# An encoder block on one core: a tile of blocks in its own buffer, p's columns loaded by pairs, and stores of y from GpSimd's queue

## The chip, the core and the metric

The kernel runs on one core of a Trainium2 chip. The metric is the device time of one execution in microseconds (us); the median of several runs is compared. Five engines work from queues of their own: TensorE (PE, matmuls and transposes), VectorE (DVE), ScalarE (ACT), GpSimd (POOL) and SyncE (SP). SP issues most of the DMAs, in the order of its queue; an instruction at the head of a queue that waits holds back all behind it.

## What is computed

Two sequences (512 prompt tokens and 1,024 sample tokens, 1,024 channels, all fp32) go through one encoder layer with the same parameters:

```python
xn = rmsnorm(h, norm_mix_g);  z = xn @ w_in                # q, k, v, g_att, u, g_f
att = diff_attention(q, k, v, lam, rel_bias)               # 4 heads, two softmaxes each
att = rmsnorm(att, subln_g, 1e-5) * (1 - lambda_init) * silu(g_att)
fno = fourier_mix(u, w_fourier) * silu(g_f)                # 2-D DFT, real part, linear map
h = h + concatenate([att, fno]) @ w_out
h = h + sigmoid(rmsnorm(h, ple_norm_g) @ w_ple_gate) * (p @ w_ple_proj)
y = rmsnorm(h, final_norm_g)
```

The change lies in the last three lines: the output projection, the gate with the per-layer input p (256 columns per token), and the final norm.

## The kernel before

Each fp32 product is made of three fp32r matmuls: an operand is split into a high part (a cast on ACT) and a low part (a subtraction on DVE), and `hi*hi + hi*lo + lo*hi` is summed in PSUM. The 1,536 tokens make twelve rows of 128 (t = 0 to 3 prompt, 4 to 11 sample).

**Stages.** First come the input projections (to about 300 us) with the Fourier part, then attention head by head, with the remaining projections filled in between its steps (`all_fill`, L586, a generator that `pour` advances). The last things in that filling are the output projection of rows 0 and 1, done plainly (`project`, L569). What remains of the output projection, rows 2 to 11, is done after attention, two rows at a time (`project_pair`, L805), and then the gate, again two rows at a time (`front`, L881, and `gate_pair`, L944).

**A pair** is a 2x2 block product in Winograd's form: seven products of 128x512 by 512x512 instead of eight (`product`, L525: 12 matmuls each, 84 a pair). Its left operand is four blocks: c11 and c12 are the two halves of the first row's columns, c21 and c22 those of the second row's. Sums of them (`s1` to `s4`) are made on DVE, and each is split on ACT and DVE. The seven products go to four PSUM banks, and DVE adds each to the row x. Some banks are summed on after DVE has read them, so a product can wait for an addition to x. A finished row is stored to the DRAM buffer `hs[t]` and its sum of squares taken (`keep`, L559).

**The blocks' buffers.** `load_cl` (L535) loads a row's two blocks from `cT` with two DMAs of 256 KB, into two tags, `hi` and `lo`, of two buffers each (2 KB per partition each). Rows 0 and 1 take all four. Row 2 (the first pair's first row) gets its two when row 0's product is done, row 3 when row 1's is done: L609 is reached once for each of t = 0 and t = 1. Rows of x lie in the tag `x` of the pool `wo` (three buffers of 4 KB per partition), each fourth row in a fourth buffer (`row`, L792). Row 2's x is loaded in `all_fill` (L611).

**The gate.** `rows_in` (L859) loads one row x back from `hs[t]`, and its 128 columns of p (`p_cols`, 128 KB, in runs of 512 B) into one buffer `pr`, and splits them into `ph` and `pl` (two buffers each). `front` scales the row by its norm on ACT into a buffer `hn` (`normed`, L868; four buffers, shared with raw weights), turns it on PE (`turn`, L874), and makes the seven operands; the block called `al11` lies in the tag `lo`. `gate_pair` does the seven products and the four products with p (`per_layer`, L907). `finish_row` (L923) makes 1/rms (the power is done on POOL, L557), multiplies on DVE into the `hn` buffer (L933), and stores y from it in two halves of 256 KB (L935). The row's x buffer is free for the load of row t+4 once DVE has read it; the `hn` buffer is free for `normed` of row t+4 once the store of y has landed.

**Order.** The framework puts the instructions of each engine in an order of its own, from priorities and estimated times, and inserts the waits; it is not always the order of the program.

Of the kernel before, what the change touches and what calls it, by code (L numbers as in the profile page):

```python
# [10 lines left out]
F32 = mybir.dt.float32  # L11
F32R = mybir.dt.float32r
# [4 lines left out]
P = 128  # L17
KB = 8
# [4 lines left out]
NT = TT // P  # L23
# [9 lines left out]
def block_kernel(ctx, tc, i, yp, ys):  # L33


    nc = tc.nc
# [16 lines left out]
    def split(hi, lo, src, hi_eng="act", lo_eng="dve"):  # L53
        if hi_eng == "act":
            a = nc.scalar.copy(out=hi, in_=src)  # L55
        else:
            a = nc.vector.tensor_copy(out=hi, in_=src)
        eng = nc.vector if lo_eng == "dve" else nc.gpsimd
        return a, eng.tensor_tensor(out=lo, in0=src, in1=hi.bitcast(F32), op=ALU.subtract)  # L59
# [11 lines left out]
    qs, kh, kl, vv, ga, uu, yT, cT = {}, {}, {}, {}, {}, {}, {}, {}  # L71
# [14 lines left out]
    hs = [dram.tile([P, D], F32, name=f"hs{t}") for t in range(NT)]  # L86
# [6 lines left out]
    def x_rows(t):  # L93
        return i["x_prompt"][0, t * P:(t + 1) * P, :] if t < 4 else \
            i["x_sample"][0, (t - 4) * P:(t - 3) * P, :]
# [17 lines left out]
    ph = ctx.enter_context(tc.tile_pool(name="ph", bufs=1, reuse_waits="tile"))  # L113
# [139 lines left out]
    with tc.tile_pool(name="pn", bufs=1, side="right", reuse_waits="tile") as pn:  # L253
# [11 lines left out]
        def load_x(t):  # L265
            x = pn.tile([P, D], F32, tag="f4", name="x", bufs=5)
            return x, nc.sync.dma_start(out=x, in_=x_rows(t))
# [32 lines left out]
        for t in range(NT):  # L300
# [8 lines left out]
            lo = ph.tile([P, 512], F32R, tag="lo", name="lo", bufs=2)  # L309
# [33 lines left out]
        first = blocks(["k0", "q0"])  # L343
# [6 lines left out]
        for t in range(NT):  # L350
            ps = nat(t, wu)
            s, r = rows_of(t)
            u = px.tile([P, 512], F32, tag="th", name="u", bufs=3)
# [153 lines left out]

    wo, small = None, None
    wb = {}
    pair_cl, x2 = [], []  # L510

    def open_out():
        nonlocal wo, small
# [4 lines left out]
    def wblock(n, tag):  # L518


        pool = wo if tag[0] == "t" else pw
        wb[n] = tuple(pool.tile([P, 4, 512], F32R, tag=tag.replace("*", z), name=f"w{n}{z}") for z in "hl")
        return wb[n]
# [8 lines left out]
    def f4(name):  # L532
        return wo.tile([P, D], F32, tag=name, name=name, bufs=3)

    def load_cl(t, pair=False):  # L535
        cl = []
        for u in range(t, t + 2 if pair else t + 1):
            c, r = u // 4, (u % 4) * P
            for z, tag in enumerate(("hi", "lo")):
                cl.append(ph.tile([P, 4, P], F32R, tag=tag, name="cl", bufs=2))  # L540
                nc.sync.dma_start(out=cl[-1].bitcast(F32), in_=cT[c].rearrange(
                    "(k p) t -> p k t", p=P)[:, 4 * z:4 * z + 4, r:r + P])
        return cl
# [42 lines left out]
    def all_fill():  # L586
        yield from blocks(["k2", "q2", "g2", "k3", "q3", "g3"])
        yield from blocks(["f0", "f1", "f2", "f3"], (0, 1))
        last = blocks(["f0", "f1", "f2", "f3"], (2,))
        for n in ("11", "12", "21", "22"):  # L590
            wblock(n, f"x*{int(n[0]) - 1}{int(n[1]) - 1}")
        for k in range(KB):
            raw = px.tile([P, D], F32, tag="raw", name="raw", bufs=2)
            nc.sync.dma_start(out=raw, in_=i["w_out"][0][k * P:(k + 1) * P, :])
            for z in range(2):
                wh, wl = wb[f"{k // 4 + 1}{z + 1}"]
                split(wh[:, k % 4], wl[:, k % 4], raw[:, 512 * z:512 * z + 512],
                      lo_eng=("dve", "pool", "dve")[k % 3])
            next(last)
            yield  # L600
        early = [load_cl(t) for t in range(2)]
        yield from last
        open_out()
        for t in range(2):
            yield from project(t, early[t], load_x(t))
            if t == 0:
                for n in ("t4", "t1"):
                    load_sums(n)
            pair_cl.extend(load_cl(t + 2))  # L609
            yield  # L610
        x2.append(load_x(2))  # L611
        load_sums("t2")
        load_sums("t3")

# [165 lines left out]
    with ExitStack() as pcx:  # L780
        pool = pcx.enter_context(tc.tile_pool(name="pc", bufs=1, side="right", reuse_waits="tile"))
# [10 lines left out]
        def row(t):  # L792
            return pool.tile([P, D], F32, tag="x", name="x") if t % 4 == 3 else f4("x")
# [51 lines left out]
        for t in range(2, NT, 2):  # L845
            if t == 4:
                wp = [[pool.tile([P, D], F32R, tag=f"wp{k}{n}", name=f"wp{k}{n}") for n in "hl"]
                      for k in range(2)]
                gfin = pool.tile([P, D], F32, name="gfin")
                nc.scalar.dma_start(out=gfin, in_=i["final_norm_g"].rearrange(  # L850
                    "(a d) -> a d", a=1).broadcast_to([P, D]))
                for k in range(2):
                    raw = raw4()
                    nc.sync.dma_start(out=raw, in_=i["w_ple_proj"][0][k * P:(k + 1) * P, :])
                    split(*wp[k], raw)
            project_pair(t, pair_cl if t == 2 else load_cl(t, True),
                         [x2[0] if t == 2 else load_x(t, row(t)), load_x(t + 1, row(t + 1))])

        def rows_in(t):  # L859
            x = row(t)  # L860
            nc.sync.dma_start(out=x, in_=hs[t])
            pr = pool.tile([P, 2, P], F32, tag="pr", name="pr", bufs=1)
            nc.sync.dma_start(out=pr, in_=i["p_cols"].rearrange("(k p) t -> p k t", p=P)[:, :, t * P:(t + 1) * P])
            p2 = [pool.tile([P, 2, P], F32R, tag=f"p{n}", name=f"p{n}", bufs=2) for n in "hl"]
            split(*p2, pr)
            return x, p2

        def normed(t, x):  # L868
            hn = raw4()
# [9 lines left out]
            return bank.rearrange("p (a b) -> p a b", b=P)  # L879

        def front(t, rows=None):  # L881
            (xa, pa), (xb, pb) = rows or (rows_in(t), rows_in(t + 1))
            ga_, gb = normed(t, xa), normed(t + 1, xb)
            a = {n: halves(n) for n in SUMS}
            f21, f11 = (ph.tile([P, 4, P], F32, tag="hi", name="c", bufs=2) for _ in range(2))
            a["11"] = a["11"][0], ph.tile([P, 4, P], F32R, tag="lo", name="al11", bufs=2)
            f1, f2 = tmp(), tmp()
            nc.scalar.copy(out=f11, in_=turn(ga_, 0, tr()))
            split(*a["11"], f11)
            ps = turn(ga_, 1, tr())  # L890
            split(*a["12"], ps)
            nc.vector.tensor_tensor(out=f2, in0=ps, in1=f11, op=ALU.add)
            nc.scalar.copy(out=f21, in_=turn(gb, 0, tr()))
            ps = turn(gb, 1, tr())
            split(*a["22"], ps)
            add(f1, f21, ps)
            split(*a["s1"], f1)

            sub(f2, f2, f1)
            split(*a["s4"], f2)  # L900
            sub(f1, f1, f11)
            split(*a["s2"], f1)
            sub(f11, f11, f21)
            split(*a["s3"], f11)
            return (xa, xb), (pa, pb), (ga_, gb), a
# [17 lines left out]
        def finish_row(t, u, x, g, ss, n):  # L923
            x, g, last = x[u], g[u], t + u == NT - 1
            rs = pool.tile([P, 1], F32, tag="rs", name="rs", bufs=2)
            nc.vector.tensor_reduce(out=rs, in_=ss[:, 4 * u:4 * u + n], op=ALU.add, axis=mybir.AxisListType.X)
            rpow(rs, rs)
            t += u
            for z in range(2):
                w = slice(512 * z, 512 * z + 512)  # L930
                dst = yp[0, t * P:(t + 1) * P, w] if t < 4 else ys[0, (t - 4) * P:(t - 3) * P, w]
                if not last:
                    nc.vector.scalar_tensor_tensor(out=g[:, w], in0=x[:, w], scalar=rs, in1=gfin[:, w],  # L933
                                                   op0=ALU.mult, op1=ALU.mult)
                    nc.sync.dma_start(out=dst, in_=g[:, w])  # L935
                elif z == 0:
                    nc.scalar.mul(out=g[:, w], in_=x[:, w], mul=rs)
                    nc.scalar.dma_start(out=dst, in_=g[:, w])
                else:
                    nc.vector.tensor_scalar(out=g[:, w], in0=x[:, w], scalar1=rs, scalar2=None,  # L940
                                            op0=ALU.mult)
                    nc.sync.dma_start(out=dst, in_=g[:, w])
# [45 lines left out]
            finish_row(t, 1, x, g, ss, 3 if last else 2)  # L988


        first = [rows_in(t) for t in range(2)]
        for n, tag in (("11", "x*00"), ("21", "x*10"), ("t4", "t4*"), ("t1", "t1*"), ("t2", "x*01"),
                       ("22", "x*11"), ("t3", "t3*")):
            if n == "t1":
# [1 line left out]
            w = wblock(n, tag)  # L996
            for k in range(0, 4, 2):
# [11 lines left out]
                for m in range(2):  # L1009
                    g = gcol[:, 4 * j + k + m:4 * j + k + m + 1]  # L1010
# [79 lines left out]
```

## Time and profile before

| | us |
|---|---|
| median of 3 runs | 961.65 (960.3 to 963.35) |
| the profiled execution's own time | 964.62 |
| its span, first to last instruction | 962.8 |
| PE busy | 915.3 (95%) |
| VectorE busy | 637.5 (66%) |
| ScalarE busy | 449.6 (47%) |
| GpSimd busy | 98.5 (10%) |

The profile is of one execution. Times in its rows count from the span's start. A row in the timeline has start, duration, engine, line, operation, output<-inputs, and in brackets how long the engine had been idle before, and what ended that. The clock that TensorE was granted is given as a share of its full speed.

### The profile page before, as it was taken

The numbers are of one execution on the slowest core, as the hardware profiler recorded it, in microseconds if no ns is written. First come the engines' busy times: TensorE is split into PE (matmuls) and PEld (weight loads), VectorE is DVE, ScalarE is ACT, GpSimd is POOL, SyncE is SP. The second block draws the span as 40 slices with busy tenths as digits, with TensorE's granted clock in tenths as the row PEclk, the third lists the DMA queues.
The fourth block names the chain that finished last, engine by engine and source line by source line (L and its number), as shares of the span: only waits on it lengthen the run. The fifth ranks groups of instructions, "written<-read, shape, count | busy, mean of one in ns | idle before, by whom it ended". The sixth has DMA issues, their size and how long they took to land.

```text
span 962.8 us, 13087 instructions
## 1 busy us (share of the span) xinstructions
PE 915.3 (95%) x4536; PEld 747.7 (78%) x4536; DVE 637.5 (66%) x1230; ACT 449.6 (47%) x908; POOL 98.5 (10%) x123
## 2 busy tenths in 40 slices
PE   5999999999999999999999999899899998999995
PEld 4788888888887788888877887777678876777774
DVE  4676443057845698597776978973676777767674
ACT  5543311032324475365554656752343566555542
POOL 3100001010000111000112122421000000000000
PEclk9999999999999999999999999999899999999998
DMA  8669889255547844753577567648875471233211
GB/s 296 226 204 338 290 273 316 85 153 154 164 139 208 228 132 150 202 158 94 180 205 213 166 171 249 195 173 312 290 242 183 143 231 55 93 99 99 93 49 44
DMA packets 123315, 175.63 MB, mean 182 GB/s; under 512 B 9385, under 2 KB 76713, under 8 KB 122225
## 3 DMA queue, kind: packets, MB, share of 16 engines
q1 hardware_dynamic: 121280, 170.72, 55.7%
q0 software_dynamic: 1392, 2.63, 0.9%
q10 hardware_dynamic: 576, 1.44, 0.5%
q8 instruction: 36, 0.59, 0.3%
q14 instruction: 31, 0.25, 0.1%
HBM read 114.96 MB, written 59.80 MB: 182 GB/s over the span
## 4 chain that ended last, share of the span: by engine, by line
PE 72%; DMA 10%; DVE 9%; ACT 4%; issue 2%; SPq 1%; POOL 1%; POOLq 0%; DVEq 0%; ACTq 0%
PE acc L147 23%; PE bank L528 11%; PE sc L657 6%; PE acc L66 6%; PE acc L68 6%; PE acc L67 6%; PE tr L684 3%; DMA x<-hs 2%; DMA raw<-sg 2%; PE tr L67 2%; PE tr L66 2%; PE tr L68 2%; PE tr L414 1%; DMA raw<-w_in 1%; PE tr L284 1%
## 5 line engine op out<-in xcount | busy, mean ns | idle before, releaser
L147 PE MATMUL acc<-xh,wch 128*128 128x512 f32 x384 | 152.2, 396 | 0.0
L147 PE MATMUL acc<-xl,wch 128*128 128x512 f32 x384 | 152.1, 396 | 0.0
L147 PE MATMUL acc<-xh,wcl 128*128 128x512 f32 x384 | 151.7, 395 | 0.0
L663 ACT ACTIVATE pt<-pt,mx 128x1024 f32<-128x1024 f32 (+1 forms) x96 | 96.5, 1007 | 62.4 <-DVE mx L660 61.8
L660 DVE CUSTOM_DVE_ANT_0 pt<-sc,tb 128x1024 f32<-128x1024 f32 (+1 forms) x96 | 97.8, 1041 | 20.3 <-PE sc L657 13.6
L147 PEld LDWEIGHTS acc<-xh,wch 128*128 128x128 f32 x384 | 72.2, 188 | 13.7 <-issue 0.2
L147 PEld LDWEIGHTS acc<-xh,wcl 128*128 128x128 f32 x384 | 72.2, 188 | 13.4
L147 PEld LDWEIGHTS acc<-xl,wch 128*128 128x128 f32 x384 | 72.2, 188 | 13.1 <-issue 0.2
L66 PE MATMUL acc<-wnh,xh 128*128 128x512 f32 x192 | 77.1, 402 | 0.5 <-ACT wnh L55 0.5
L67 PE MATMUL acc<-wnl,xh 128*128 128x512 f32 x192 | 76.8, 400 | 0.0
L68 PE MATMUL acc<-wnh,xl 128*128 128x512 f32 x192 | 76.2, 397 | 0.0
L657 PE MATMUL sc<-kk,qq 128*128 128x512 f32 x160 | 65.7, 411 | 2.4 <-DMA kh_p<-hi 1.6
L657 PE MATMUL sc<-kll,qq 128*128 128x512 f32 x160 | 63.9, 399 | 0.0
L55 ACT CAST wth<-tr 128x512 fp32r<-128x512 f32 x80 | 45.4, 582 | 32.0 <-PE tr L684 31.8
L59 DVE TENSOR_TENSOR wtl<-tr,wth 128x512 fp32r<-128x512 f32 x80 | 53.5, 685 | 6.5 <-ACT wth L55 6.4
L679 DVE SCALAR_TENSOR_TENSOR pt<-pt,rc,pt 128x1024 f32<-128x1024 f32 (+1 forms) x48 | 56.0, 1166 | 1.1
L684 PE MATMUL tr<-ident,pt 128*128 128x128 f32 x320 | 48.4, 276 | 5.8 <-DVE g L729 4.2
L684 PEld LDWEIGHTS tr<-ident,pt 128*128 128x128 f32 x320 | 36.6, 140 | 17.1 <-DVE g L729 6.7
L705 POOL TENSOR_TENSOR g<-ot,g 128x256 f32<-128x256 f32 x24 | 20.3, 847 | 287.6 <-ACT ot L704 282.3
L66 PE MATMUL tr<-wth,v 128*128 128x256 f32 x160 | 45.6, 285 | 0.2 <-DVE wtl L59 0.2
L67 PE MATMUL tr<-wtl,v 128*128 128x256 f32 x160 | 45.5, 284 | 0.3 <-DVE wtl L59 0.2
L68 PE MATMUL tr<-wth,v 128*128 128x256 f32 x160 | 45.1, 282 | 0.0
(297 smaller groups left out, 2056.7 us busy)
## 6 DMA issues: line engine op xcount, KB each, us to landing
raw<-w_in SPq DMA_DIRECT2D x28, 512.0 KB, 5.1
x<-x_sample SPq DMA_DIRECT2D x16, 512.0 KB, 4.7
sot<-o SPq DMA_DIRECT2D x16, 512.0 KB, 4.1
cl<-cT SPq DMA_DIRECT2D x24, 256.0 KB, 3.8
hs<-x SPq DMA_DIRECT2D x12, 512.0 KB, 4.4
x<-hs SPq DMA_DIRECT2D x12, 512.0 KB, 3.8
x<-x_prompt SPq DMA_DIRECT2D x8, 512.0 KB, 5.2
wr<-w_out SPq DMA_DIRECT2D x8, 512.0 KB, 5.8
```

The costliest lines, as they stand in the source:

```text
L55: a = nc.scalar.copy(out=hi, in_=src)
L59: return a, eng.tensor_tensor(out=lo, in0=src, in1=hi.bitcast(F32), op=ALU.subtract)
L66: nc.tensor.matmul(out=out, lhsT=wh, rhs=xh, start=start, stop=False)
L67: nc.tensor.matmul(out=out, lhsT=wh, rhs=xl, start=False, stop=False)
L68: nc.tensor.matmul(out=out, lhsT=wl, rhs=xh, start=False, stop=stop)
L147: nc.tensor.matmul(out=ps, lhsT=a[:, k], rhs=b[c][k // 4][:, k % 4], start=(n == 0), stop=(n == 23))
L528: nc.tensor.matmul(out=out[:, w], lhsT=a[u][:, k], rhs=b[v][:, k, w], start=(start and k == 0 and n == 0), stop=(k == 3 and n == 2), skip_ ...
L657: nc.tensor.matmul(out=pss[c][:, n:n + 512], lhsT=qq[c], rhs=k[c][:, n:n + 512], start=(m == 0), stop=(m == 1))
L660: nc.vector.tensor_tensor_reduce(out=pt[c][:, :T], in0=ps[:, :T], in1=tb[:, off:off + T], scale=-1.0, scalar=3e38, op0=ALU.add, op1=ALU.mi ...
L663: nc.scalar.activation(out=pt[c][:, :T], in_=pt[c][:, :T], func=AF.Exp, scale=-1.0, bias=mx[:, c:c + 1], accum_out=sm[:, c:c + 1])
L679: nc.vector.scalar_tensor_tensor(out=pt[0][:, :T], in0=pt[1][:, :T], scalar=rc[:, 1:2], in1=pt[0][:, :T], op0=ALU.mult, op1=ALU.add)
L684: nc.tensor.transpose(out=ps[:, j * P:(j + 1) * P], in_=pt[0][:, (b + j) * P:(b + j + 1) * P], identity=ident)
```

## The change

Three edits. (1) After row 0's product, `all_fill` loads row 2's blocks as before, and row 3's two blocks with one DMA of 512 KB into a buffer of the tag `x` instead of into `hi` and `lo`; row 2's x is loaded in the pair's own step rather than in `all_fill`. (2) `rows_in` handles a pair of rows: it loads both rows x, reserves the gate's `al11` in the tag `lo`, and loads the pair's 256 columns of p with one DMA (runs of 1 KB) into the other `lo` buffer. (3) The stores of y of rows 0 to 9 are issued by GpSimd, those of rows 10 and 11 as before.

```diff
-    pair_cl, x2 = [], []
+    pair_cl = []
...
-            pair_cl.extend(load_cl(t + 2))
+            if t == 0:
+                pair_cl.extend(load_cl(2))
+                whole = wo.tile([P, KB, P], F32, tag="x", name="c3", bufs=3)
+                nc.sync.dma_start(out=whole, in_=cT[0].rearrange("(k p) t -> p k t", p=P)[:, :, 3 * P:4 * P])
+                pair_cl.extend([whole[:, 0:4], whole[:, 4:8]])
             yield
-        x2.append(load_x(2))
         load_sums("t2")
         load_sums("t3")
...
             project_pair(t, pair_cl if t == 2 else load_cl(t, True),
-                         [x2[0] if t == 2 else load_x(t, row(t)), load_x(t + 1, row(t + 1))])
+                         [load_x(t, row(t)), load_x(t + 1, row(t + 1))])
 
         def rows_in(t):
-            x = row(t)
-            nc.sync.dma_start(out=x, in_=hs[t])
-            pr = pool.tile([P, 2, P], F32, tag="pr", name="pr", bufs=1)
-            nc.sync.dma_start(out=pr, in_=i["p_cols"].rearrange("(k p) t -> p k t", p=P)[:, :, t * P:(t + 1) * P])
-            p2 = [pool.tile([P, 2, P], F32R, tag=f"p{n}", name=f"p{n}", bufs=2) for n in "hl"]
-            split(*p2, pr)
-            return x, p2
+
+            x = [row(t), row(t + 1)]
+            for u in range(2):
+                nc.sync.dma_start(out=x[u], in_=hs[t + u])
+            al11 = ph.tile([P, 4, P], F32R, tag="lo", name="al11", bufs=2)
+            pr = ph.tile([P, 2, 2 * P], F32, tag="lo", name="pr", bufs=2)
+            nc.sync.dma_start(out=pr, in_=i["p_cols"].rearrange("(k p) t -> p k t", p=P)[
+                :, :, t * P:(t + 2) * P])
+            p2 = []
+            for u in range(2):
+                p2.append([pool.tile([P, 2, P], F32R, tag=f"p{n}", name=f"p{n}", bufs=2) for n in "hl"])
+                split(*p2[u], pr[:, :, u * P:(u + 1) * P])
+            return x, p2, al11
...
-            (xa, pa), (xb, pb) = rows or (rows_in(t), rows_in(t + 1))
+            (xa, xb), (pa, pb), al11 = rows or rows_in(t)
...
-            a["11"] = a["11"][0], ph.tile([P, 4, P], F32R, tag="lo", name="al11", bufs=2)
+            a["11"] = a["11"][0], al11
...
-                    nc.sync.dma_start(out=dst, in_=g[:, w])
+                    (nc.gpsimd if t < NT - 2 else nc.sync).dma_start(out=dst, in_=g[:, w])
...
-        first = [rows_in(t) for t in range(2)]
+        first = rows_in(0)
```

## Rows read from the trace of the kernel before

**Rows 1.** Busy time by stretch: us, each engine's busy us, PE's granted clock, DMA share, GB/s
```profile
680.00:700.00 20.00, 18.76 (x68) 14.63 (x69) 15.46 (x24) 8.21 (x14) 0.00 (x0) 0.83 0.77 260
720.00:740.00 20.00, 20.00 (x89) 16.30 (x88) 13.03 (x23) 7.21 (x16) 1.64 (x3) 1.00 0.52 171
```

**Rows 2.** Timeline of PE, 655 to 720 us: the matmuls that it was idle before
```profile
672.58 0.49 PE L528 MATMUL bank<-w21h,ah 128*128 128x512 f32 x1 [1.82 <-ACT ah L55]
679.02 0.50 PE L528 MATMUL bank<-wt4h,ah 128*128 128x512 f32 x1 [2.62 <-ACT ah L55]
680.50 0.50 PE L528 MATMUL bank<-wt4h,al 128*128 128x512 f32 x1 [0.75 <-DVE al L59]
683.51 0.80 PE L528 MATMUL bank<-w11h,cl 128*128 128x512 f32 x1 [0.74 <-DVE cl L59]
701.53 0.50 PE L528 MATMUL bank<-w11h,cl 128*128 128x512 f32 x1 [0.84 <-DVE cl L59]
```

**Rows 3.** The chain that ended last: start, us, what
```profile
672.53 5.79 DMA cl<-cT
...
690.15 7.12 DMA pr<-p_cols
...
701.53 60.75 PE bank L528 x262
```

**Rows 4.** Busy time in the first pair's products (84 matmuls)
```profile
672.58:700.06 27.48, 23.35 (x84) 17.50 (x85) 17.73 (x27) 10.10 (x17) 0.45 (x1) 0.88 0.83 284
```

**Rows 5.** Timeline of SP's queue around the first pair
```profile
657.55 1.00 SPq L551 DMA_DIRECT2D x<-x_prompt  x2
...
664.80 0.38 SPq L541 DMA_DIRECT2D cl<-cT  x1
...
672.53 0.45 SPq L541 DMA_DIRECT2D cl<-cT  x1
```

**Rows 6.** DMA issues from 674.3 to 675.6 us: number, KB each, us to landing
```profile
x<-x_prompt SPq DMA_DIRECT2D x1, 512.0 KB, 7.8
```

**Rows 7.** Timeline of ACT at the first load of p
```profile
697.30 0.41 ACT L55 CAST ph<-pr 128x256 fp32r<-128x256 f32 x1 [2.15 <-DMA pr<-p_cols]
```

**Rows 8.** Tile pr, 640 us to the end: its other split, min/median/max ns
```profile
L59 DVE TENSOR_TENSOR pl<-pr,ph x12: 415/418/426, 697.7 to 928.0; 128x256 fp32r<-128x256 f32 x12
```

**Rows 9.** What PE waited for from 800 us on: us, times, longest
```profile
PE tr L877 <- ACT raw L870: 7.0, 5, 3.4
```

**Rows 10.** Timeline of PE, 840 to 865 us: the matmul that it was idle before
```profile
858.74 1.96 PE L877 MATMUL tr<-ident,raw 128*128 128x128 f32 x8 [1.94 <-ACT raw L870]
```

**Rows 11.** Busy time just behind that wait
```profile
860.00:862.00 2.00, 2.00 (x8) 1.71 (x7) 0.65 (x2) 1.05 (x2) 0.00 (x0) 0.50 0.00 0
```

**Rows 12.** The chain that ended last, 815 to 836 us
```profile
826.82 1.43 DVE raw L933 x2
...
828.27 0.33 SPq L935
...
828.70 3.88 DMA x<-hs
```

**Rows 13.** The chain that ended last, at row 7's load
```profile
852.22 5.15 DMA x<-hs
```

**Rows 14.** The stores of y by SP: landing
```profile
DMA to landing us min/median/max: 2.0/2.2/2.5
```

**Rows 15.** A load of 192 KB that POOL issued, min/median/max ns, and its landing
```profile
L489 POOL DMA_DIRECT2D tcph<-tabc_p x1: 567/567/567, 163.1 to 163.1; - x1
...
DMA to landing us min/median/max: 7.4/7.4/7.4
```

**Rows 16.** Another load that POOL issued (L240, 128 KB): its landing
```profile
DMA to landing us min/median/max: 3.8/3.8/3.8
```

**Rows 17.** Busy time by stretch, at the load of rows 15 and in the gate
```profile
163.00:171.00 8.00, 8.00 (x36) 6.44 (x35) 0.00 (x0) 0.59 (x1) 1.17 (x3) 1.00 0.95 279
...
828.00:833.00 5.00, 5.00 (x23) 4.04 (x22) 2.37 (x5) 1.40 (x4) 0.00 (x0) 1.00 0.74 236
```

## The prediction

> **What bounds the kernel now.** I began with the busy time by stretch. PE is busy all through the steady pairs of the output projection, at full clock, and DVE has a third of its time free there [rows 1]. So PE's own work sets the end, and only what stops PE or slows its clock can be won; the change removes no matmul. I then went through PE's timeline for the places where it stood idle behind the last transposes of attention. There are five before 720 us, all at the first pair of the output projection and at the start of the next [rows 2], and in the stretch around them the granted clock falls to 0.83 on average, full speed before and after [rows 1]. From 800 us on PE waits five times for the scaled row that it has to turn [rows 9]. The chain that ended last says what stands behind the first group: the load of the last block of row 3, then the load of p's columns, and then PE alone for 60 us [rows 3]. SP's queue says why the block is late: row 3's first block is issued at 664.80, the second at 672.53 [rows 5], since its buffer is held until row 1's product ends.
>
> **The change, part by part**
>
> **Row 3 in a buffer of its own.** The wait of that load for row 1's buffers goes. The third buffer of the tag x was free early: row 2's x went into it, in one of the two loads at 657.55 [rows 5]. Row 3's blocks can take that place, some 15 us ahead of 672.53. Price of the delay: the first pair's 84 matmuls took 27.48 us from first to next pair [rows 4]. In the undisturbed run 262 matmuls took 60.75 us, 0.232 us each [rows 3]; 84 of them are 19.5 us. The loss is 27.5 - 19.5 = 8.0 us: three waits of 2.62, 0.75 and 0.74 [rows 2] are 4.1 of it, and the remaining 3.9 are matmuls at the low clock and restarts. PE fell to the lower of its levels (1.2 GHz) after these waits, and no other reason for it shows. I take all 8.0 as won. The wait of 1.82 ahead of the pair [rows 2] I leave: it ends with the cast of row 2's block, whose load was issued before 657.55. Lower end of the gain: 4.1, if the clock still falls.
>
> What is late next? Row 2's x. Its load moves from 657.55 to the pair's own step, beside row 3's x, and that one, issued between 674.3 and 675.6, took 7.8 us to land [rows 6]; so about 682. DVE adds the third product to it, and the fifth product waits for this addition. The first product starts at 672.58; four products of 12 x 0.232 = 2.8 us end at 683.7. Row 2's x with an addition of some 0.7 us is ready at 682.8. It fits with 1 us to spare, so I cost it at nothing; if the load is 3 us later it costs 2. The 512 KB move ahead of other loads and are missing later, so the DMA total stays. Row 4's x now waits for row 3's blocks to be used, which is over before its own load is reached.
>
> **The next pair's start.** Its wait of 0.84 (about 1.0 with the restart) ends with a DVE split [rows 2]. In the chain ACT stood 2.15 us at the head of its queue for p's load, which took 7.12 us, and the casts that pair needed were behind it [rows 3, 7]. The first loads of p leave this stretch, and the pair's blocks come earlier. I take 1.0 as won; bounds 0 and 1.0.
>
> **p by pairs.** One DMA in place of two, the same bytes. The first pair's columns can be loaded only when the last projection pair has used its `lo` blocks. So two casts of 0.41 on ACT and two subtractions of 0.42 on DVE [rows 7, 8] move from a stretch where neither engine set the pace into the one where the gate's weights are split, and that one ends with PE's longest wait, 3.4 us [rows 9]. Bounds: nothing, if they fall into idle time; 1.7 if all four lie in a row. I take 0.8, one engine's two. In later pairs nothing waits: `al11` gives up a buffer, but its partner for the high part has only one anyway.
>
> **y from GpSimd.** In SP's queue the load of row t+4 stands behind the second store of row t: DVE ends at 826.82 + 1.43 = 828.25, the store is issued at 828.27, the load at 828.70, and it lands 3.88 later [rows 12]. Without the store the load goes out 0.43 earlier. That shortens the four waits that follow this pattern, 7.0 - 3.4 = 3.6 us together [rows 9]: 4 x 0.43 = 1.7. At most all four go, with the low clock behind the longest of them: 1.94 us idle, then 2 us at 0.50, worth about 1.3 [rows 10, 11]; 4.9 in all. But `normed` also waits until y has left its buffer. By SP that was 2.2 us [rows 14]. A store by GpSimd is not in the trace; the nearest rows are loads that GpSimd issued: 0.57 us of POOL each, and 3.8 or 7.4 us to landing [rows 15, 16]. The 7.4 fell into a stretch in which the DMA engines were busy for 0.95 of the time; at the gate's loads it is 0.74 [rows 17]. So I take 3.8, and keep 7.4 for the slower rival. It equals the 3.88 of the row's load, so nothing is lost. On POOL the stores wait for DVE; behind them stands only the power of the next row, whose input DVE makes later.
>
> The Trainium skill speaks against this: SBUF, State Buffer, section "SBUF: two separate sides", says that descriptors of a DMA from GpSimd cannot be written while DVE runs certain copies, and gives 3.1 us in place of 0.62. The landing would be 3.8 + 2.5 = 6.3 us, an estimate from that page, and the sum worse by some 2 us a pair, 8 in all. The instructions behind y's multiplication in this trace are additions and subtractions of two tensors, which that page does not put among them; no run here shows the case.
>
> **Sum.** -8.0 - 1.0 + 0.8 - 1.7 = -9.9 us against the profiled execution's 964.62, that is 954.7. The runs' median is 961.65, 3.0 below it; I take the same difference off: 951.8 us.
>
> **The rivals**
>
> **Something else holds the first pair.** Row 2's x, or the queue of loads behind it, is late by 3 to 4 us, and the clock falls again. For it: 7.8 us to landing [rows 6]. Against: 1 us of room, and more if the scheduler places the load as soon as row 0's buffer is stored. Gain of row 3's buffer then 4, in all 5 to 6: 956.
>
> **The block's load is not sooner.** The order of SP's queue is the framework's; were the load still issued around 672, only the rest remains: -1.0 + 0.8 - 1.7 = -1.9, 959.8. Against: two loads went out at 657.55 [rows 5], one of them into this very buffer.
>
> **Slower: y lands late.** If stores by GpSimd take 7.4 us [rows 15], `normed` starts 7.4 instead of 4.33 us after DVE (828.25 to 828.70 + 3.88), 3.1 later, in three of the four places, and 1.8 later at row 7, whose load took 5.15 [rows 12, 13]: 11.1 us of PE idle, with the low clock (1.3 us, as behind the one wait that is long now) at three more places, 3.9. Against a gain of 8.2 from the other two parts that is +6.8: 968.4. It decides once y lands more than 4.33 + 8.2/4 = 6.4 us after DVE's end.
>
> **How the numbers follow.** Forecast 0.72, late x 0.13, not sooner 0.07, y late 0.08. A measurement of this kernel can tell 0.3%, 2.9 us, from no change. The forecast and late x are faster by more: 0.85. Not sooner is within it: 0.07. Slower 0.08. Range: from 947.0 (all of the four gate waits and the low clock won and p free: -9.0 - 4.9 = -13.9, 947.8, and a little of the 1.82) to 958.0 (the gain of the clock lost, 4.1, and p at 1.7, y winning nothing: -3.4, 958.2). It leaves out the last two rivals and few of the rest.
>
> **What would show it.** Right: row 3's blocks loaded before 665; no waits of PE between 673 and 695 beside short ones, and a granted clock of 1.00 there; the next pair's products some 8 to 9 us earlier, and that distance kept to the end; SP's queue with loads of x directly behind DVE's multiplication; PE's waits at L877 shorter by some 0.4 each. Wrong: a wait of PE for an addition to x in the first pair; ACT waiting for p at the head of its queue between 750 and 775; `normed` waiting for a store of y, and PE's waits at L877 longer than before.

## The result, and the profile after

The changed kernel takes 972.70 us (median of 5 runs, 971.53 to 973.69), the kernel before 961.88 (5 runs, 960.3 to 963.71). The ratio is 1.011, interval 1.0093 to 1.0128: slower by 10.8 us, where 9.9 us less were forecast. What came is the rival in which y lands late. In the changed kernel `turn` is L886, `normed` L879, the load of x L866, y's multiplication L942, its store L944.

**Where the time went, by stage.** The stores of rows to `hs` divide the run. Their first and last start (min/median/max ns of the issue ahead of them), in the kernel before and then in the changed one:

```profile
L561 SPq DMA_DIRECT2D hs<-x x12: 319/326/411, 655.3 to 782.0; - x12
```

```profile
L561 SPq DMA_DIRECT2D hs<-x x12: 320/330/390, 656.7 to 778.3; - x12
```

With the spans, 962.8 and 970.9 us: up to the first store +1.4, from first to last 126.7 and 121.6, so -5.1; from the last to the end 180.8 and 192.6, so +11.8. Against this one execution of the kernel before, the output projection won half of what was forecast for it, and the gate lost more than twice that. The first of the two sizes is uncertain: in the run `c_only` below, whose code is that of the kernel before up to the stores of y, the first and the last start are 123.8 us apart (655.0 to 778.8), so the changed kernel's 121.6 is 2.2 to 5.1 shorter.

**The output projection.** Changed kernel, PE's timeline from 670 to 682 us, the matmuls that it was idle before; then busy time in the first pair's products and in the next pair's (columns as in [rows 1]).

```profile
674.94 0.51 PE L528 MATMUL bank<-w21h,ah 128*128 128x512 f32 x1 [2.78 <-ACT ah L55]
677.02 0.51 PE L528 MATMUL bank<-w11h,ah 128*128 128x512 f32 x1 [0.62 <-ACT ah L55]
...
678.55 0.63 PE L528 MATMUL bank<-w21h,ah 128*128 128x512 f32 x1
```

```profile
674.94:697.13 22.19, 21.57 (x84) 16.87 (x85) 16.86 (x26) 10.06 (x18) 0.46 (x1) 0.92 0.97 339
697.13:716.51 19.38, 19.38 (x86) 15.79 (x84) 13.69 (x27) 7.28 (x17) 2.03 (x3) 1.00 0.75 255
```

The three waits inside the first pair are gone [rows 2], one of 0.62 stands there, and it takes 22.19 us instead of 27.48 [rows 4]. Both stretches differ between executions of one code, though. In `c_only` they are:

```profile
672.29:698.45 26.16, 23.48 (x85) 17.45 (x85) 18.99 (x30) 11.01 (x20) 0.46 (x1) 0.87 0.87 299
698.45:717.82 19.37, 19.37 (x85) 15.79 (x84) 14.06 (x27) 7.39 (x17) 2.14 (x3) 1.00 0.79 269
```

There PE waited 2.32 and 0.25 us inside the first pair, and not at all at the next pair's start. In `ab`, which has all of the change but the stores, the two stretches take 21.99 and 20.52 us. In the changed kernel the wait ahead of the first pair is 2.78 instead of 1.82, and behind it the matmuls run slowly: 0.63 us each, a granted clock of 0.92 over the pair. The engines ahead of PE say why the wait grew. Changed kernel, DVE's and then ACT's timeline there:

```profile
671.28 0.69 DVE L583 TENSOR_TENSOR x<-x,acc 128x512 f32<-128x512 f32 x1 [3.88 <-PE acc L68]
671.89 0.68 DVE L803 TENSOR_TENSOR tmp<-tmp,cl 128x512 f32<-128x512 f32 x1
...
672.89 0.68 DVE L583 TENSOR_TENSOR x<-x,acc 128x512 f32<-128x512 f32 x1
```

```profile
673.66 0.60 ACT L564 ACTIVATE acc<-x 128x512 f32<-128x512 f32 x1 [0.93 <-DVE x L583]
...
674.29 0.60 ACT L55 CAST ah<-cl 128x512 fp32r<-128x512 f32 x1
```

With row 3's blocks there early, a subtraction of the pair (L803) can run, and it does so between the halves of row 1's last addition (L583). The second square of row 1 on ACT waits 0.93 us for the second half, and the cast that PE waits for stands behind that square.

**The gate.** Changed kernel: what PE waited for from 800 us on (us, times, longest), then `normed` on ACT (busy us, mean ns | idle ahead of it, releasers), and the same of the kernel before:

```profile
PE tr L886 <- ACT raw L879: 16.0, 9, 2.8
```

```profile
L879 ACT ACTIVATE raw<-x,small 128x1024 f32<-128x1024 f32 x12 | 13.7, 1146 | 20.7 <-DMA y_sample<-raw 10.4 <-DMA y_prompt<-raw 10.0 <-issue 0.3
```

```profile
L870 ACT ACTIVATE raw<-x,small 128x1024 f32<-128x1024 f32 x12 | 13.7, 1148 | 10.2 <-DMA x<-hs 9.9 <-issue 0.3
```

PE waits 16.0 us in 9 places, where it was 7.0 in 5 [rows 9], and `normed` waits eight times for a store of y, where it had always waited for x. ACT stands 20.4 us at it in all instead of 9.9, and what is behind it in ACT's queue comes later too: from 800 us on DVE's sum of a row's squares waits 13.1 us for ACT, 6.0 before. The stores of y in the changed kernel, min/median/max us from issue to landing:

```profile
DMA to landing us min/median/max: 2.0/4.9/5.3
```

From SP it was 2.0/2.2/2.5 [rows 14]. One row (row 1) in detail, changed kernel, timelines of DVE, SP, POOL, ACT and PE:

```profile
821.73 1.41 DVE L942 SCALAR_TENSOR_TENSOR raw<-x,rs,gfin 128x512 f32<-128x512 f32 x2 [0.77 <-POOL rs L557]
...
823.22 0.32 SPq L866 DMA_DIRECT2D x<-hs  x1
...
823.03 1.12 POOL L944 DMA_DIRECT2D y_prompt<-raw  x2 [1.33 <-ACT raw L930]
...
828.93 1.15 ACT L879 ACTIVATE raw<-x,small 128x1024 f32<-128x1024 f32 x1 [5.05 <-DMA y_prompt<-raw]
...
830.13 1.12 PE L886 MATMUL tr<-ident,raw 128*128 128x128 f32 x8 [2.73 <-ACT raw L879]
```

DVE ends at 821.73 + 1.41 = 823.14. The load of row 5's x goes out at 823.22, POOL is busy with the two stores until 824.15. What the DMA queues moved then (q1 holds SP's transfers, q0 POOL's: packets, MB, share of 16 engines), in 824.5 to 826 and in 826 to 827.5:

```profile
q1 hardware_dynamic: 68, 0.28, 71.5%
```

```profile
q0 software_dynamic: 112, 0.40, 65.5%
q1 hardware_dynamic: 63, 0.19, 31.7%
```

Until 826 only the load moves; the stores move when it is nearly over, and `normed` starts 5.8 us after DVE's end, where it was 4.3 before [rows 12]. Behind the wait the clock falls here too: 0.91 over 820 to 840 us, where it had been 1.00.

For rows 8 and 9, whose y is stored by GpSimd without a load of x beside it (no row t+4 is left), the landing is another. Changed kernel, DMA issues from 943.8 to 945 us, then what moved from 943.9 to 945.4:

```profile
y_sample<-raw POOLq DMA_DIRECT2D x2, 256.0 KB, 2.5
```

```profile
q0 software_dynamic: 39, 0.16, 27.4%
```

So GpSimd's stores alone land in 2.5 us; their first packets move at about 945.0, 1.1 us after the issue at 943.86. The framework also put PE's instructions in another order in the gate. Row 8's turns, for one, stand in the changed kernel in the midst of the product with w21 and wait 2.21 us; in the same kernel with y on SP (the run `ab` below) they stand 17 matmuls later, in the product with wt4, and wait for nothing. PE's timeline of the changed kernel and of `ab`:

```profile
875.48 0.40 PE L528 MATMUL bank<-w21l,ah 128*128 128x512 f32 x1
878.08 1.28 PE L886 MATMUL tr<-ident,raw 128*128 128x128 f32 x8 [2.21 <-ACT raw L879]
```

```profile
868.20 0.39 PE L528 MATMUL bank<-wt4h,ah 128*128 128x512 f32 x1
868.45 1.09 PE L886 MATMUL tr<-ident,raw 128*128 128x128 f32 x8
```

### The profile page after: what moved, and what is told of

Its sections match the earlier page's. It is cut to its first block, busy times and chain, and to the rows that moved or that the text cites. A ratio compares the mean times of both kernels' runs of the same rounds, so it can differ in the third digit from the quotient of the medians.

```text
span 970.9 us, 13078 instructions
## 1 busy us (share of the span) xinstructions
PE 918.4 (95%) x4536; PEld 750.0 (77%) x4536; DVE 637.4 (66%) x1230; ACT 449.7 (46%) x908; POOL 109.9 (11%) x143
```

## The experiments

Three causes were to be told apart in the gate: the store of y stands behind the load of x on the DMA engines; GpSimd's queue is slow by itself; the turns stand earlier in PE's queue. Ratios are against the kernel before on the same chip (its medians there: 959.92, 961.0 and 962.24 us); runs are compared by ratios, and 0.001 is about 1 us.

**`c_only`: only the stores move.** The kernel before, with one line of the change:

```diff
-                    nc.sync.dma_start(out=dst, in_=g[:, w])
+                    (nc.gpsimd if t < NT - 2 else nc.sync).dma_start(out=dst, in_=g[:, w])
```

> The kernel before with the stores of y by GpSimd alone. Theory (y lands late, because the load of row t+4 now goes ahead of it, and normed waits for y): the whole loss of the gate, some 12 us, shows here: 974 us, between 971 and 978, with some 16 us of PE waiting for the scaled row from 800 us on and y landing 4.5 to 5.5 us after its issue. Rival (the loss comes from p's or al11's new buffers): no change, 960 to 964, and y lands no later than 3.

Measured: 978.43 us, ratio 1.0189 (1.0164 to 1.0214). The turns' group of that kernel (busy, mean ns | idle ahead of it):

```profile
L877 PE MATMUL tr<-ident,raw 128*128 128x128 f32 x96 | 14.6, 297 | 20.2 <-ACT raw L870 19.7 <-ACT c L888 0.5
```

The time is 0.4 above the theory's upper end, the waits are 19.7 us where some 16 were expected, and y lands after 4.8 us at the median, within the range given. This line alone makes the kernel 18 us slower; the other parts of the change do not cause the loss, they hide 8 us of it.

**`ab`: all but the stores.** The changed kernel with y stored by SP:

```diff
-                    (nc.gpsimd if t < NT - 2 else nc.sync).dma_start(out=dst, in_=g[:, w])
+                    nc.sync.dma_start(out=dst, in_=g[:, w])
```

> The changed kernel with the stores of y back on SP. Theory: the gain before the gate stays (row 8's store came 5.5 us earlier, counted from row 0's store) and the gate costs what it cost before: 956.5 us, between 954 and 959. Rival (p's or al11's buffers cost the gate its time): 966 or more.

Measured: 954.91 us, ratio 0.9946 (0.9929 to 0.9963), the landing of y 2.1 us, and:

```profile
L886 PE MATMUL tr<-ident,raw 128*128 128x128 f32 x96 | 13.3, 279 | 2.9 <-ACT raw L879 1.7 <-ACT c L897 1.1
```

Faster than both kernels. Against the changed kernel it is 1.011 - 0.9946 = 0.0164, some 16 us.

**`a_only`: only row 3's blocks in a buffer of their own.** The kernel before, with L612 to L614 of the changed one, row 2's x in the pair's step, and p and y as they were:

```diff
-            pair_cl.extend(load_cl(t + 2))
+            if t == 0:
+                pair_cl.extend(load_cl(2))
+                whole = wo.tile([P, KB, P], F32, tag="x", name="c3", bufs=3)
...
-        x2.append(load_x(2))
```

> The kernel before with row 3's blocks in their own buffer alone. Theory: nearly all of the gain before the gate is this part's: 957 us, 955 to 959; the rest, up to 1 us, is p's load that no longer holds ACT at the second pair. Rival (p by pairs brings the gain): above 960.

Measured: 954.97 us, ratio 0.9945 (0.9929 to 0.9961), at the lower end of the theory's range. It equals `ab`: all the gain is this part's, and the loads of p by pairs bring and cost nothing that can be measured.

**`after_hn5`: no wait for y's buffer.** The changed kernel with a fifth buffer of the tag that `normed` and y use; to make room, the final norm's gain is left out, and y is multiplied by split weights of p in its place.

```diff
-            return pool.tile([P, D], F32, tag="hn", name="raw", bufs=4)
+            return pool.tile([P, D], F32, tag="hn", name="raw", bufs=5)
...
-                gfin = pool.tile([P, D], F32, name="gfin")
...
+                gfin = wp[0][0].bitcast(F32)
```

> The changed kernel with five buffers hn instead of four, so that normed of row t+4 takes a buffer whose y was stored one row earlier; to make room the final gain's buffer is left out and y is multiplied by the split weights of p instead. Theory: normed no longer waits for a store; PE's waits for the scaled row from 800 us on fall from 16.0 to below 6 us, the time to 955 to 960, although y lands as late as before. Rival (the loads themselves are slower beside GpSimd's stores, or POOL's power is late): the waits stay above 12 and the time above 967.

Measured: 961.11 us, ratio 1.0022 (1.0008 to 1.0035), y landing in 4.8 us as before the edit:

```profile
L877 ACT ACTIVATE raw<-x,small 128x1024 f32<-128x1024 f32 x12 | 13.7, 1148 | 13.8 <-DMA x<-hs 12.8 <-DVE w22l L1019 1.0
L884 PE MATMUL tr<-ident,raw 128*128 128x128 f32 x96 | 13.4, 279 | 10.1 <-ACT raw L877 9.9 <-ACT c L895 0.2
```

With y as late as ever, 0.0088 (8.5 us) come back when nobody waits for its landing, although the framework put the turns 56 matmuls further forward in all than in the changed kernel. But the time is 1.1 above the theory's upper end, and the turns still wait 9.9 us, not the under 6 that were expected, for rows that now wait for x; so more than y's buffer is at work.

**`ab_hn5`: its control.** The same five buffers, y on SP.

```diff
-            return pool.tile([P, D], F32, tag="hn", name="raw", bufs=4)
+            return pool.tile([P, D], F32, tag="hn", name="raw", bufs=5)
...
-                    (nc.gpsimd if t < NT - 2 else nc.sync).dma_start(out=dst, in_=g[:, w])
+                    nc.sync.dma_start(out=dst, in_=g[:, w])
```

> y stored by SP, but with five buffers of the tag that y, normed and x share, so that normed waits for no store of y; the gain gfin is left out here (y is multiplied by a buffer of split weights in its place) to make room. It is the control of the changed kernel with five buffers (961.1): what is left between the two is what GpSimd's stores cost apart from the wait for y. Theory (the store's landing is what counts): with y on SP the wait for y is under 2 us already, so five buffers bring at most 2 us: 951 to 956. Rival (normed's buffer is what holds the gate whatever queue y takes): 945 to 950.

Measured: 954.07 us, ratio 0.9921 (0.9891 to 0.995), against 0.9946 (0.9929 to 0.9963) with four: the intervals overlap, so the fifth buffer brings little or nothing where y goes by SP, as the theory had it. Between the two kernels with five buffers there is still 0.0101, some 10 us, with nobody waiting for y. In the one with GpSimd's stores the load of x lands after 4.5 us at the median of the gate's eight, in the other after 3.8, and the turns stand earlier in PE's queue, by one to seven matmuls. Two runs below take the place of the turns by itself; how the 10 us divide here is not shown.

**`after_xpool`: stores first again.** The changed kernel with the load of x on GpSimd too, behind the stores:

```diff
-                nc.sync.dma_start(out=x[u], in_=hs[t + u])
+                nc.gpsimd.dma_start(out=x[u], in_=hs[t + u])
```

> The changed kernel with the loads of x from hs in the gate stage also issued by GpSimd, behind the two stores of y, so that stores and loads share one queue again and the stores go first, as on SP before. Theory (a store of y is late because a 512 KB load of the row four further on, issued on another queue about when the row's y is multiplied, takes the DMA engines ahead of it): y lands 2.3 to 3 us after its issue instead of the 4.9 median, normed's waits for y fall from 20.4 us in all to under 4, and the time is 954 to 962 us. Rival (a store issued by GpSimd is slow by its queue, whatever runs beside it): y's landing stays at 4.5 us or more and the time at 968 to 976. Rival (the order of the turns in PE's queue, which the framework chose for the changed kernel): the waits of the turns for ACT stay at 12 us or more although y lands early.

Measured: 962.87 us, ratio 1.0012 (0.9996 to 1.0028), just above the theory's upper end. The landing of y, then of x:

```profile
DMA to landing us min/median/max: 2.0/2.4/4.0
...
DMA to landing us min/median/max: 3.9/4.7/6.8
```

Same queue, same stores, the same kind of instructions of DVE behind y's multiplication: y lands in 2.4 us at the median (GpSimd's stores 2.3 to 4.0) once the load stands behind it. That GpSimd's stores land late whatever runs beside them is excluded. `normed` waits for x now, 8.7 us, since two issues of POOL (0.56 us each) stand ahead of the load, and the load itself takes 4.7 from there, by SP 3.7 in `ab` (medians of the gate's eight loads).

The time says less than the landing. `normed` starts 4.9 to 6.5 us behind DVE's end here, no sooner than in the changed kernel (4.9 to 5.8), so the some 9 us that this run wins over it do not come from an earlier scaled row. In this kernel the framework put the turns of rows 4 to 11 further back in PE's queue, by 66 matmuls in all against the changed kernel and 13 against `ab`, and PE waits 7.2 us for them instead of 16.0. No run takes that order by itself.

**`ab_xpool`: the opposite half.** y by SP, the loads of x by GpSimd:

```diff
-                nc.sync.dma_start(out=x[u], in_=hs[t + u])
+                nc.gpsimd.dma_start(out=x[u], in_=hs[t + u])
...
-                    (nc.gpsimd if t < NT - 2 else nc.sync).dma_start(out=dst, in_=g[:, w])
+                    nc.sync.dma_start(out=dst, in_=g[:, w])
```

> y stored by SP as before the change, and only the loads of x from hs issued by GpSimd: the opposite half of the move. Theory of order on shared engines: with two queues whichever transfer is issued first goes first; GpSimd has no work of the row ahead of the load, so the load starts as early as in the changed kernel and stands ahead of the stores again: y lands at 4 to 5 us, normed waits for y, and the time is 966 to 976, near the changed kernel's 972. Rival (GpSimd's queue is slow for stores alone): y lands at 2.3 us from SP, the time is that of the kernel with y on SP, 953 to 957.

Measured: 965.91 us, ratio 1.0061 (1.0038 to 1.0083). The time is just under the expected range, the reason is not the expected one: y lands in 2.1 us, and it is x that is late.

```profile
L879 ACT ACTIVATE raw<-x,small 128x1024 f32<-128x1024 f32 x12 | 13.8, 1148 | 16.5 <-DMA x<-hs 16.2 <-issue 0.3
```

SP's first store goes out when the first half is multiplied, the load only when both are, so with SP at the stores the load can't pass them. Issued by GpSimd about 0.5 us behind DVE's end, as by SP in `ab`, it lands after 4.1 us instead of 3.7 (medians of the gate's eight loads). So the load, too, is later by GpSimd than by SP. That is not all of the 11 us between the two kernels: the turns, too, stand 38 matmuls further forward here than in `ab`.

**`after_ord` and `ab_ord`: the order of PE's queue alone.** The list of the gate stage's matmuls and turns, as it stands in the one kernel, is imposed on the other by dependencies without waits. The edit is the same in both; only the list differs, and y's queue is each kernel's own:

```diff
+                mm = nc.tensor.transpose(out=bank[:, j * P:(j + 1) * P], in_=hn[:, k * P:(k + 1) * P],
...
+                rec.setdefault(lab, []).append(mm.ins)
...
+        for run in ORDER.split():
+            lab, n = run.split(":")
+            for _ in range(int(n)):
+                ins = rec[lab].pop(0)
+                if last is not None:
+                    tc.add_manual_dep(ins, last.name, mybir.DependencyInfo(
+                        mybir.DependencyClass.NoSync, mybir.DependencyReason.DATA), reason="order")
+                last = ins
```

> The changed kernel with PE's order in the gate stage held to that of the kernel with y on SP (954.9): eight of the turns of a pair's rows stand 53 matmuls further back in all, 53 x 0.232 = 12.3 us; nothing else is edited, y is stored by GpSimd. Theory (two causes of the 17.8 us between 972.7 and 954.9: y in its buffer until 5.3 to 5.8 us behind DVE's end in place of 4.2, and turns that the framework put earlier in PE's queue): normed still starts 5.3 to 5.8 us behind DVE, the turns' waits for ACT fall from 16.0 to 4 to 9 us, and the time is 960 to 968. Rival (the place of the turns does not matter, since what follows them would wait for the same rows): 970 to 975, the wait moves from the turns to the products behind them. Rival (the place is nearly all of it): 954 to 959.

> The mirror of it: y stored by SP, and PE's order in the gate stage held to that of the changed kernel, turns early. Theory (two causes): normed starts 4.0 to 4.5 us behind DVE as with y on SP, but the turns wait for it 7 to 12 us in all in place of 1.7, and the time is 960 to 967, near the 961.1 of the changed kernel with five buffers. Rival (the place does not matter): 953 to 957.

Measured: `after_ord` 968.58 us, ratio 1.0073 (1.0048 to 1.0099), 0.6 above the theory's upper end; `ab_ord` 961.65, 0.9994 (0.9973 to 1.0014), inside its range. The turns in `after_ord` and in `ab_ord`:

```profile
L901 PE MATMUL tr<-ident,raw 128*128 128x128 f32 x96 | 14.3, 292 | 13.4 <-ACT raw L893 11.9 <-ACT c L913 1.5
```

```profile
L901 PE MATMUL tr<-ident,raw 128*128 128x128 f32 x96 | 13.4, 279 | 7.1 <-ACT raw L893 5.8 <-ACT c L913 1.3
```

With `ab` and the changed kernel this is a square, ratios to the kernel before:

| | turns as in `ab` | turns as in the changed kernel |
|---|---|---|
| y by SP | 0.9946 | 0.9994 |
| y by GpSimd | 1.0073 | 1.011 |

The queue of y costs 0.0127 and 0.0116, 11 to 12 us; the place of the turns 0.0048 and 0.0037, 3.5 to 4.6 us. The two add up. The second is close to the noise: with y by SP the two intervals are apart by 0.001, with y by GpSimd they overlap by 0.0006. A cost of the imposed list itself would lower one of these two figures and raise the other, and they differ by 0.0011. Of the rivals of `after_ord`, the place is not all (954 to 959). That it is nothing (970 to 975) is missed by 1.4 us only, less than the noise of that run; `ab_ord` speaks against it, 961.65 where 953 to 957 had been given.

`normed` starts 5.1 to 5.9 us behind DVE's end in `after_ord` and 4.0 to 4.9 in `ab_ord`, as expected of either. PE's waits for the scaled row grow with the times: 1.7 us in `ab`, 5.8 in `ab_ord`, 11.9 in `after_ord`, 16.0 in the changed kernel. Both expectations of these waits missed, 11.9 where 4 to 9 had been given and 5.8 where 7 to 12 had; the place of the turns is a minor cause. Only PE's order is held; what the framework did to ACT's is in these figures too.

**`ab_keep2`: can the first pair's wait be shortened?** `ab`, with row 1's squares on ACT behind the casts of the first pair:

```diff
+            if t == 2:
+                with tc.issue_after(cast.ins):
+                    keep(1, late[0])
```

> The kernel with the early blocks and y on SP (954.9), with row 1's statistics moved on ACT behind the casts of the first output pair's operands. Theory (in the changed kernel the first pair's products wait 2.78 us and then run at a low clock because ACT does row 1's squares ahead of the cast of ah, and those squares wait for the second half of DVE's addition): the wait falls under 1.9 us, the low clock of 677.7 to 680.7 is gone, and the time is 951 to 953.5. Rival (the wait is set by DVE, whose subtraction of the pair stands between the halves of the addition): the wait stays between 2.3 and 2.8 us and the time within 954 to 956.

Measured: 956.55 us, ratio 0.9958 (0.994 to 0.9977), `ab` 0.9946: no gain. PE's timeline of it in the first pair:

```profile
673.71 0.50 PE L528 MATMUL bank<-w21h,al 128*128 128x512 f32 x1 [1.59 <-DVE al L59]
677.32 0.50 PE L528 MATMUL bank<-w11h,cl 128*128 128x512 f32 x1 [1.25 <-DVE cl L59]
...
691.14 0.47 PE L528 MATMUL bank<-w22h,ahs 128*128 128x512 f32 x1 [2.29 <-DVE x L809]
```

The 2.78 us have become 1.59 + 1.25 = 2.84, now for DVE: the rival was right that DVE sets this start, though wait and time lie just above its ranges. The low clock did go, 1.00 over 660 to 680 where `ab` has 0.91, and it brought nothing to the median. In this execution a new wait of 2.29 us stands later in the pair: an addition to x is late on DVE, which had stood 5.09 us at the split of p's weights, whose load was late. Whether the other executions had it is not shown.

## Why the prediction was wrong, step by step

**The sign.** It hung on one sentence of the step "y from GpSimd": the landing of 3.8 "equals the 3.88 of the row's load, so nothing is lost". The step took the stores out of SP's queue and let the load start 0.43 us earlier, and it priced the store alone. What it left out is that the two then compete, and which goes first changes. On SP the two stores went first and x, the longer, was what `normed` waited for. From two queues the load goes first, and `normed` waits for it and then for y. Both transfers are needed before `normed` can start, so taking the store off the load's way won nothing; the last of the two ended later. In the trace `normed` started 4.1 to 4.5 us behind DVE's end in six of eight rows before, and 5.3 to 5.8 us in seven of eight after (row 4, behind row 0: 4.9). The landing that the step put at 3.8 measured 4.9 at the median, and POOL's own issues, for which it counted nothing, put the second store's end of issue at 824.15, 1.0 us behind DVE's end in row 1. The term of -1.7 measured +16 us (the changed kernel against `ab`), 11 to 12 of them with the turns held in place.

The Trainium skill says in DMA: Bandwidth & Descriptors, section "Issuing engines are not separate DMA queues", that DMAs started by different engines run on the same 16 engines and interleave, and that starting them from several saves only the issue time. The trace agrees on the shared engines (65.5% and 31.7% of the 16 for the two queues in 826 to 827.5 us) and that no more than the issue time was to be had (the load went out 0.08 us behind DVE's end in row 1 instead of 0.45). On the interleaving it agrees only in part: from 826 us both queues move, but until then no packet of the stores did.

**The slower rival** had the mechanism (y in its buffer) and the sign, but gave 968.4 and needed y to land more than 6.4 us behind DVE's end. It counted three or four waits, the odd rows'. There are eight, since the even rows had little slack: PE waits at nine turns. And 3.5 to 4.6 us of the loss do not come from y's landing, but from the framework: with the stores elsewhere it put the turns earlier in PE's queue. The prediction named the framework's order as a risk for one load, not for PE.

**The Trainium skill's warning** in the prediction, a landing of 6.3 us because of DVE, is not what happened: the same kind of instructions of DVE stand behind y in `after_xpool`, and y lands in 2.4 us at the median. The landing of 4.9 lies between the two figures, for another reason.

**Row 3 in a buffer of its own.** The direction held: the three waits are gone, row 3's blocks were loaded at 658.95 instead of 672.53. The term of 8.0 measured 27.48 - 22.19 = 5.3, inside its bounds of 4.1 to 8.0. It was read from one execution, and a slow one: `c_only` took 26.16 for the first pair with the same code, and against that the term is 4.0, just under the lower bound. What failed besides is that the wait of 1.82 ahead of the pair was left as it is: it became 2.78 (1.0 lost), and the low clock stayed, behind this wait instead of the later ones. The last of it is DVE's: earlier operands let DVE's work of the pair run ahead of what ACT needs. Row 2's x was late as costed (DVE waits for it until 683.48), and PE did not wait: nothing, as the step had it.

**The next pair's start.** The -1.0 is not borne out. The stretch took 19.38 us instead of 20.52 before (700.06 to 720.58), but it took 19.37 in `c_only`, with the old loads, and 20.52 in `ab`, with the new ones. So the time lost there comes and goes between executions, and that the profiled changed kernel lost none can't be put down to the change.

**p by pairs.** +0.8 was too high: `ab` and `a_only` differ by 0.06 us, well inside their intervals.

**Sum.** Without the stores -8.2 were forecast, and `ab` measured 0.0054 of 960, -5.2. The first two pairs with the wait ahead of them took 45.3 us in `ab` and 43.8 in `a_only`; against 49.8 in the profiled run before that is 4.5 and 6.1 less, against 47.4 in `c_only` 2.1 and 3.6 less. So these pairs hold a part of the 5.2, and how much is not shown. That the profiled `a_only` and `ab` are also 5 to 7 us shorter in the gate than the profiled run before (180.8 us; 175.9 and 174.1) does not show in the medians; the run profiled before was some 3 us above its median, and the rest of that difference stays open.

## What to carry to other kernels

A buffer's next user waits for the last of all transfers it needs. Before a transfer is moved to another queue, list what its old queue put behind it, and ask which of them the next step needs last; two queues give no more DMA engines, they only give up the order. And a change of queue can make a scheduling framework reorder an engine that the change does not touch, so compare the engines' orders before the times are read.

## What the runs showed of the hardware

- A 256 KB store by GpSimd costs 0.56 us of POOL, lands in 2.3 to 2.5 us without a load of x beside it (the changed kernel's rows 8 and 9), and, as the second of its row, in 4.5 to 5.3 us with a 512 KB load by SP issued within 0.5 us of it (rows 0 to 7).
- While that load moved, GpSimd's queue moved nothing (824.5 to 826 us), though the load's share of the engines was 0.715. Why the free rest was not used is open.
- In the gate a load of 512 KB by GpSimd lands in 4.1 us (`ab_xpool`) to 4.7 us (`after_xpool`) at the median, by SP in 3.7 (`ab`).
- POOL issued its first store 1.30 us after DVE had begun the row (821.73 to 823.03); SP in `ab` did so in 0.78 (818.37 to 819.15).
